# Choosing the order of 30 experts on the chip: a routed feed-forward layer whose weights are loaded from addresses in registers

## The chip, the core and the metric

The kernel runs on one core of one Trainium2 chip. The metric is the device time of one execution in microseconds (us). The core has a matrix engine (PE, with its weight loads shown apart as PEld), three other compute engines (DVE, ACT, POOL), an engine that issues transfers (SP), and 16 DMA engines that carry what SP, ACT and POOL issue. Operands lie in on-chip memory; the experts' weights lie in HBM and are read once.

## The reference

One decoder layer on 512 rows of width 1024. A mixing sublayer (pooling, RWKV-7, mLSTM, an output projection) makes `h`; it isn't touched here. Then comes a routed feed-forward sublayer with 32 experts, of which each row uses four:

```python
logits = xt @ router_w + router_b
top_val, top_idx = lax.top_k(logits, 4)
gate = jax.nn.softmax(top_val, axis=-1)
# for each expert e, over the rows that chose it:
gu = xb @ w_gu[e] + b_gu[e]                      # 1024 x 2048 weights
glu, lin = jnp.minimum(gu[:, :1024], 7.0), jnp.clip(gu[:, 1024:], -7.0, 7.0)
y_e = (glu * jax.nn.sigmoid(1.702 * glu) * (lin + 1.0)) @ w_dn[e] + b_dn[e]   # 1024 x 1024 weights
# y = sum over the four experts of gate * y_e
h = layer_norm(DEEPNORM_ALPHA * h + y, ln2_g, ln2_b)
```

With the inputs used here the experts have these numbers of rows, from expert 0 to expert 31: 69, 59, 80, 37, 61, 63, 63, 79, 48, 57, 64, 74, 77, 68, 68, 59, 75, 67, 61, 69, 39, 62, 77, 46, 60, 46, 71, 54, 74, 88, 51, 82. Fifteen of them have more than 64 rows; they are called heavy below, the other 17 light.

## The kernel before

The mixing sublayer fills the first 380 us or so. After it the program holds 32 expert steps, written out one behind the other in the order 0 to 31 (`experts`).

**Weights.** Each expert's weights are 12 chunks of 1 MiB: eight of `w_gate_up` (`load_gu`) and four of `w_down` (`load_dn`). SP issues them (L1193) into a ring of 18 buffers, in the order: gate_up of 0, gate_up of 1, down of 0, gate_up of 2, down of 1, and so on; down of 30 and down of 31 come last. An issue waits for the matmuls that read its buffer before, and, since there are eight completion lanes for SP's transfers, for the landing of the transfer eight places ahead of it. So the time of an issue that waits for a DMA is the time at which the chunk eight places ahead has landed. The addresses are constants of the program.

**Matmuls.** An expert's gathered rows (`expert_gather`, POOL, L1217) are transposed on PE; rows 0 to 63 are multiplied in `gu_low` (L1285) and in the first part of `dn` (L1331), whatever the number of rows. Rows 64 to 95 are done in `gu_high` (L1290) and `high` (L1326) only if the expert has more than 64 rows: a branch on a count, which PE, ACT and POOL each load into a register (`fill`). Experts 0 and 31 have no branch and always do both parts. `dn` of expert e runs behind the gate_up product of expert e + 1.

**Outputs.** `out` scales a result on ACT (L1335) and POOL adds it to the rows of `yd` in HBM by an indirect transfer (L1336): one for rows 0 to 63, one more for rows 64 to 95 of a heavy expert. Expert 31 is an exception: its result stays on chip (`slast`), split in a high and a low part.

**Tail.** When the additions of expert 30 have landed, POOL issues four transfers `res<-yd` (L1529, `tail_rows`), one for each block i of 128 rows, which add `yd` onto the residual `res[i]`. `tail` then does for each block: one-hot matmuls that put `slast` at its rows (L1545, L1548); for blocks 2 and 3 also a product of `res[i]` with the identity (L1543), so that PE does the addition; blocks 0 and 1 are added on DVE (L1560). Then the layer norm on ACT and DVE (L1558 to L1577) and the stores (L1578). The program text goes through the blocks from 0 to 3; the scheduler that builds the program sets the order on each engine.

**Expert 0.** While its gate_up product runs, PE also does the routing: `route_counts` (L1094, the counts of all experts by products with ones), `route_table` (L1128, the rows of each expert, by 16 products with one-hot matrices `S`), `tables` (L1174), and `out_init` for four blocks (L1140 a transpose, L1147 the down biases). `S` lies in a buffer of the ring, and the transposes and biases free others, so SP's first loads behind gate_up of expert 1 wait for these matmuls.

Of the kernel before, what the change touches and what calls it, by code (L numbers as in the profile page):

```python
# [40 lines left out]
OB = 104  # L41
PADROWS = 128

CONST_W = {}


def _consts():
    P = np.arange(128)
    cols = {}
    cols["ident"] = np.eye(128)  # L50
    strict = (P[:, None] < P[None, :]).astype(np.float64)
    incl = (P[:, None] <= P[None, :]).astype(np.float64)
# [24 lines left out]
    cols["par"] = (P[:, None] // 64 == np.arange(2)[None]).astype(np.float64)  # L77
    cols["quad"] = (P[:, None] // 32 == np.arange(4)[None]).astype(np.float64)
    cols["bd2"] = (P[:, None] // 64 == np.arange(2)[None]).astype(np.float64)
    at, parts = {}, []  # L80
    n = 0
    for k, a in cols.items():
        at[k] = (n, a.shape[1])
        n += a.shape[1]
        parts.append(a)
    return np.concatenate(parts, 1).astype(np.float32), at
# [40 lines left out]
class Trunk:  # L127
# [4 lines left out]
    def setup(self):  # L132
        nc, tc, a = self.nc, self.tc, self.a
        self.cp = cp = self.ctx.enter_context(tc.tile_pool(name="const", bufs=1))
        self.dp = self.ctx.enter_context(tc.tile_pool(name="dram", bufs=1, space=DRAM))
        self.ident = cp.tile([128, 128], F32, name="ident")
        nc.gpsimd.dma_start(self.ident, a["consts"][:, 0:128])
        self.C = cp.tile([128, CONSTS.shape[1] - 128], F32, name="cst")
        self.c = {k: self.C[:, o - 128:o - 128 + n] for k, (o, n) in CAT.items() if k != "ident"}
        e = cp.tile([128, 2], F32, name="eps")  # L140
        self.eps = {v: e[:, q:q + 1] for q, v in enumerate((1e-5, 64e-5))}
        for v, col in self.eps.items():
            nc.vector.memset(col, v)
        self.wd = self.dp.tile([6, T], F32, name="wd")
        self.tab = self.dp.tile([NE * 512, 2], F32, name="tab")
        self.hd = self.dp.tile([T + PADROWS, D], F32, name="hd")
        self.yd, self.yo = (self.dp.tile([T + PADROWS, D], F32, name=n) for n in ("yd", "yo"))

    def params(self):
        nc, a, cp = self.nc, self.a, self.sp  # L150
        self.pc = cp.tile([128, NPR], F32, name="pcol")
        nc.gpsimd.dma_start(self.pc, a["pcol"])
        nc.sync.dma_start(self.C, a["consts"][:, 128:])
# [785 lines left out]
        self.nc.scalar.dma_start(self.hd[i * 128:i * 128 + 128], r)  # L939

    def norm_params(self):
        nc, sp = self.nc, self.sp
        z = sp.tile([128, 2, 2, 128], F32, name="mkv", tag="mkv", bufs=2).rearrange("p a b c -> p (a b c)")
        self.lg = z[:, 0:128].rearrange("p (i e) -> p i e", i=NT)
        self.mk = z[:, 128:256].rearrange("p (i e) -> p i e", i=NT)
        self.v8 = z[:, 256:288].rearrange("p (i e) -> p i e", i=NT)
        self.i8 = sp.tile([128, NT, 8], U32, name="i8")
        s = self.slot("t", "ln1")
        self.lng, self.lnb = s[:, 0:1024], s[:, 1024:2048]
        for t, n in ((self.lng, "ln1_g"), (self.lnb, "ln1_b")):  # L950
            src = self.a[n]
            d = nc.scalar.dma_start(t, bass.AP(tensor=src.tensor, offset=src.offset, ap=[[0, 128], [1, D]]))
            self.after(d, self.ml_ins)
        s = self.slot("z", "slots")
# [133 lines left out]
        nc.vector.tensor_copy(self.pbs[:, i], pb)  # L1088

    def route_counts(self):  # L1090
        nc, cp = self.nc, self.cp
# [4 lines left out]
        nc.vector.tensor_copy(self.cnti, p[:, :NE])  # L1096
        self.mxi = cp.tile([128, 1], I32, name="mxi")
        mx = cp.tile([128, 1], F32, name="mx")
        nc.vector.reduce_max(mx, p[:, :NE], axis=AX.X)
        nc.vector.tensor_copy(self.mxi, mx)  # L1100


    def route_slots(self):
        nc, c = self.nc, self.c
        z = self.slot("z", "S")
# [17 lines left out]
    def route_table(self):  # L1123
        nc = self.nc
        V = self.V.rearrange("p i k e -> p (i k) e")
        p = self.tbank()
        for k in range(16):
            nc.tensor.matmul(p[0:CAP, 0:64], self.S[:, k], V[:, k], start=(k == 0), stop=(k == 15))  # L1128
        nc.vector.tensor_scalar(self.tt[:, 0:32], p[0:CAP, 0:32], self.c["pad"][0:CAP], None, OP.add)
        nc.vector.tensor_copy(self.tt[:, 32:64], p[0:CAP, 32:64])  # L1130

# [60 lines left out]
    def load(self, dst, src, gate):  # L1192
        i = self.nc.sync.dma_start(dst, src)  # L1193
        if gate is not None:
            self.after(i, gate)

    def load_gu(self, e):
        out = []
        for k in range(NK):
            w, gate = self.chunk()  # L1200
            self.load(w, self.a["w_gate_up"][e, k * 128:(k + 1) * 128], gate)
            out.append(w)
        return out

    def load_dn(self, e):
        out = []
        for k in range(0, NK, 2):
            w, gate = self.chunk()
            self.load(w.rearrange("p (k c) -> p k c", k=2), self.a["w_down"][e, k * 128:(k + 2) * 128].rearrange("(p k) c -> p k c", k=2), gate)
            out += [w[:, 0:1024], w[:, 1024:2048]]  # L1210
        return out

# [20 lines left out]

    def expert_sel(self, e):
        sel = self.mw.tile([128, 2, 128], F32R, name="sel") if e else self.cp.tile([128, 2, 128], F32R, name="sel0")
        self.nc.vector.tensor_scalar(sel[:, 0], self.c["bsel0"], 2.0 * e, None, OP.is_equal)
        self.nc.vector.tensor_scalar(sel[:, 1], self.c["bsel2"], 4.0 * e, None, OP.is_equal)  # L1237
        return sel


# [24 lines left out]


    def fill(self, e):
        if e in (0, NE - 1):
            return None
        return self.nc.values_load(self.cnti[0:1, e:e + 1], engines=[mybir.EngineType.PE, mybir.EngineType.Activation, mybir.EngineType.Pool], min_val=0, max_val=T,  # L1270
                                   skip_runtime_bounds_check_because="a count of rows, which only decides a branch")


# [90 lines left out]

    def experts(self):
        self.xg = [self.mw.tile([128, D], F32, name=f"xg{q}") for q in range(2)]
        xs, xT = {}, {0: self.first_xT()}
# [323 lines left out]
```

## Time and profile before

| | us |
|---|---|
| three timed runs | 1468.14, 1470.26, 1470.38 |
| median | 1470.26 |
| profiled execution, own time | 1465.28 |
| its span in the trace | 1463.5 |
| mean granted clock of TensorE in it | 0.976 of full |

The span is what the engines' records cover; the profiled execution's own time is 1.8 us more. All rows below come from that execution, and count from the start of its span.

### The profile page before, as it was taken

How to read it: one execution, taken by the hardware profiler on the slowest of the kernel's cores; microseconds unless marked ns; L12 is line 12 of the kernel's file. 1: busy time of each engine (PE TensorE's matmuls, PEld its weight loads, DVE VectorE, ACT ScalarE, POOL GpSimd, SP SyncE). 2: the span in 40 equal slices, each digit the busy share in tenths (PEclk: the TensorE clock that was granted, in tenths of full speed). 3: DMA queues.
4: the chain of work that ended last, by engine and by line, in shares of the span. 5: the costliest groups of instructions: out<-in, count | busy, mean ns of one | idle time of the engine just before them, and what ended most of it. 6: DMA issues, size and time to landing. Idle time of an engine off the chain costs nothing. (4 is left out here: it accounts for less than half of the span.)

```text
span 1463.5 us, 19946 instructions
## 1 busy us (share of the span) xinstructions
PE 1334.6 (91%) x7860; PEld 623.9 (43%) x7861; DVE 448.4 (31%) x1070; ACT 289.5 (20%) x617; POOL 206.8 (14%) x190
## 2 busy tenths in 40 slices
PE   7899978998999999987899999999879878899995
PEld 5677878876533333322233333333323222333323
DVE  5767687788521112111111121111111111211114
ACT  4444342453011111110001111111100100111103
POOL 1211236241001100110001111011100100010100
PEclk9999996899999999999999999999999999999998
DMA  7222233346899999999999999999999999999974
GB/s 253 73 58 72 52 79 99 132 141 269 297 364 375 396 385 403 396 390 395 403 403 397 396 398 399 406 394 394 391 389 402 394 404 395 400 395 415 408 297 118
DMA packets 95232, 461.88 MB, mean 316 GB/s; under 512 B 18084, under 2 KB 26692, under 8 KB 45962
## 3 DMA queue, kind: packets, MB, share of 16 engines
q1 hardware_dynamic: 79962, 435.61, 75.9%
q0 software_dynamic: 10592, 20.49, 6.5%
q10 hardware_dynamic: 4560, 4.15, 0.9%
q8 instruction: 82, 1.34, 0.4%
q14 instruction: 36, 0.29, 0.1%
HBM read 445.97 MB, written 18.10 MB: 317 GB/s over the span
## 5 line engine op out<-in xcount | busy, mean ns | idle before, releaser
L1285 PE MATMUL gu<-wc,xT 128*64 128x512 f32 x2048 | 486.5, 603 | 65.1 <-DMA wc<-w_gate_up 62.2
L1285 PEld LDWEIGHTS gu<-wc,xT 128*64 128x64 f32 x2048 | 143.1, 137 | 388.5 <-issue 243.1
L1298 DVE TENSOR_SCALAR glu<-gu 128x256 f32<-128x256 f32 (+1 forms) x64 | 35.6, 556 | 829.1 <-PE gu L1290 376.6
L1331 PE MATMUL dn<-wc,aT 128*64 128x512 f32 x1024 | 247.5, 603 | 4.2 <-PEq L1278 2.4
L1299 ACT ACTIVATE glu<-glu 128x256 f32<-128x256 f32 (+1 forms) x64 | 33.5, 524 | 543.1 <-DVE glu L1298 543.1
L1217 POOL DMA_INDIRECT xg<-hd,gidx x31 | 30.9, 998 | 670.8 <-PE tr L1230 660.8
L1331 PEld LDWEIGHTS dn<-wc,aT 128*64 128x64 f32 x1024 | 65.1, 136 | 118.9 <-issue 102.3
L1290 PE MATMUL gu<-wc,xT 128*32 128x512 f32 x960 | 111.5, 596 | 0.0
L1336 POOL DMA_INDIRECT yd<-eo,sidx x45 | 70.1, 1557 | 275.2 <-ACT eo L1335 275.2
L222 PE MATMUL pi<-xhi,whi 128*128 128x512 f32 x152 | 65.0, 428 | 15.9 <-ACT whi L172 8.9
L1231 ACT ACTIVATE xT<-tr 128x384 f32<-128x384 f32 x62 | 29.8, 490 | 181.1 <-PE tr L1230 181.1
L223 PE MATMUL pi<-xlo,whi 128*128 128x512 f32 x152 | 63.7, 419 | 0.5 <-DVE xlo L173 0.5
L224 PE MATMUL pi<-xhi,wlo 128*128 128x512 f32 x152 | 62.8, 413 | 0.0
L1290 PEld LDWEIGHTS gu<-wc,xT 128*32 128x32 f32 x960 | 27.0, 109 | 80.1 <-issue 79.8
L1335 ACT ACTIVATE eo<-dn,gate 128x512 f32<-128x512 f32 (+1 forms) x45 | 27.9, 621 | 163.0 <-PE dn L1331 88.9
L1326 PE MATMUL dn<-wc,aT 128*32 128x256 f32 x960 | 56.1, 381 | 1.0 <-ACT aT L1313 1.0
L173 POOL TENSOR_TENSOR wlo<-wraw,whi 128x512 fp32r<-128x512 f32 (+1 forms) x28 | 39.0, 1397 | 124.3 <-ACT whi L172 120.3
L1326 PEld LDWEIGHTS dn<-wc,aT 128*32 128x32 f32 x960 | 29.5, 110 | 34.0 <-issue 14.6
L172 ACT ACTIVATE whi<-wraw 128x512 fp32r<-128x512 f32 (+1 forms) x54 | 33.8, 634 | 47.8 <-DMA wraw<-w_in 21.9
L222 PEld LDWEIGHTS pi<-xhi,whi 128*128 128x128 f32 x152 | 30.0, 197 | 26.2 <-ACT whi L172 8.5
L1301 DVE SCALAR_TENSOR_TENSOR glu<-glu 128x256 f32<-128x256 f32 (+1 forms) x64 | 35.4, 555 | 7.2 <-ACT glu L1299 6.2
L1312 PEld LDWEIGHTS tr<-ident,glu 128*128 128x128 f32 x192 | 25.5, 208 | 26.4 <-DVE sel L1237 19.5
(489 smaller groups left out, 1501.1 us busy)
## 6 DMA issues: line engine op xcount, KB each, us to landing
wc<-w_gate_up SPq DMA_DIRECT2D x256, 1024.0 KB
wc<-w_down SPq DMA_DIRECT2D x128, 1024.0 KB
wraw<-w_in SPq DMA_DIRECT2D x46, 256.0 KB
wraw<-w_out SPq DMA_DIRECT2D x16, 256.0 KB
xraw<-xT SPq DMA_DIRECT2D x4, 512.0 KB
res<-x SPq DMA_DIRECT2D x4, 512.0 KB
hd<-res ACTq DMA_DIRECT2D x4, 512.0 KB
res<-yd POOLq DMA_DIRECT2D x4, 512.0 KB
```

Source lines behind the costliest of these rows:

```text
L172: self.hi_ins = nc.scalar.activation(hi, src, AF.Copy)
L173: return (eng or nc.vector).tensor_tensor(lo, src, hi, OP.subtract)
L222: nc.tensor.matmul(p, hi, xh, start=(k == 0), stop=False)
L223: nc.tensor.matmul(p, hi, xl, start=False, stop=False)
L224: nc.tensor.matmul(p, lo, xh, start=False, stop=(k == NK - 1))
L1285: mm(p[q][64 * h:64 * h + 64], xT[:, k, 0:64], w[:, 1024 * q + 512 * h:1024 * q + 512 * h + 512], start=False, stop=(k == NK - 1))
L1290: self.nc.tensor.matmul(p[2][32 * c:32 * c + 32], xT[:, k, 64:96], w4[:, c], start=False, stop=(k == NK - 1), skip_group_check=True)
L1298: nc.vector.tensor_scalar(out[:, c], g, 7.0, None, OP.min)
L1301: nc.vector.scalar_tensor_tensor(out[:, c], ln[:, c], 1.0, out[:, c], OP.add, OP.mult)
L1326: mm(p2[32 * c:32 * c + 32], aT[:, 4 + k % 2, 32 * (k // 2):32 * (k // 2) + 32], wd[k][:, 256 * c:256 * c + 256], start=(k == 0), stop=(k ...
L1331: mm(p0[64 * h:64 * h + 64], aT[:, k % 4, 64 * (k // 4):64 * (k // 4) + 64], wd[k][:, 512 * h:512 * h + 512], start=(k == 0), stop=(k == N ...
L1336: return nc.gpsimd.indirect_dma_start(out=self.yd.rearrange("t (c f) -> (t c) f", f=w), out_offset=bass.IndirectOffsetOnAxis(ap=self.sidx[ ...
```

## The change

The experts are put in an order by their number of rows, found on the chip. `route_counts` gets, besides the counts along a row, the counts down a column (eight small products), compares all pairs, and sums to a rank; experts 0 and 1 are kept at ranks 0 and 1. The constant `TURN` says which rank stands at which place of the program: ranks 2 to 13 alternate with ranks 14 to 25 at places 4 to 27, two others stand at places 2 and 3, and the four last ranks at places 28 to 31. With the counts above, the places have, from 0 to 31: 69, 59, 48, 51, 88, 68, 82, 67, 80, 64, 79, 63, 77, 63, 77, 62, 75, 61, 74, 61, 74, 60, 71, 59, 69, 57, 68, 54, 46, 46, 39, 37 rows. So four heavy ones stand at places 4 to 7, and from there on heavy and light ones take turns; the last four places are light.

A one-hot matrix `turn` gives the expert's number and its count for each place (`permi`) and brings the table of rows and gates into the new order by one more product. SP loads an expert's number into a register for each place from 2 on (`turn_of`) and adds it to the address of each chunk. The biases' selection compares with a column of `perm` instead of a constant. The last place now has the branch too.

```diff
+TURN = [0, 1, 27, 26] + [r for n in range(12) for r in (2 + n, 14 + n)] + [28, 29, 30, 31]
...
     def route_counts(self):
...
+        for g in range(2):
+            for i in range(NT):
+                nc.tensor.matmul(p[32 * g:32 * g + 32, 64:65], self.mkb[:, i], self.onesb[:, 0:1], start=(i == 0), stop=(i == NT - 1))
+        z = self.zS
+        key, col, self.turn, self.ttT = z[:, 1536:1568], z[0:64, 1568:1572], z[0:64, 1576:1640], z[0:64, 1640:1736]
+        no = z[0:NE, 1736:1864]
+        nc.vector.tensor_scalar(no, self.onesb[0:NE], self.cno[0:NE], None, OP.mult)
+        nc.vector.tensor_tensor(key, p[:, :NE], self.ctie, OP.add)
+        nc.vector.tensor_copy(col[:, 0:1], p[0:64, 64:65])
+        nc.vector.tensor_tensor(col[:, 1:2], col[:, 0:1], self.ctiec[0:64], OP.add)
+        nc.vector.tensor_scalar(self.turn[:, 0:NE], key[0:64], col[:, 1:2], None, OP.is_gt)
+        nc.vector.reduce_sum(col[:, 2:3], self.turn[:, 0:NE], axis=AX.X)
+        nc.vector.tensor_scalar(self.turn, self.cturn[0:64], col[:, 2:3], None, OP.is_equal)
+        q = self.tbank()
+        nc.tensor.matmul(q[:, 0:NE], no, self.turn[0:NE, 0:NE], start=True, stop=True)
+        nc.tensor.matmul(q[0:1, 64:64 + NE], col[0:NE, 0:1], self.turn[0:NE, 0:NE], start=True, stop=True)
...
     def route_table(self):
...
-            nc.tensor.matmul(p[0:CAP, 0:64], self.S[:, k], V[:, k], start=(k == 0), stop=(k == 15))
+            nc.tensor.matmul(p[0:64, 64:64 + CAP], V[:, k], self.S[:, k], start=(k == 0), stop=(k == 15))
+        tt = self.ttT
+        nc.vector.tensor_copy(tt, p[0:64, 64:64 + CAP])
+        nc.tensor.matmul(p[0:CAP, 0:64], tt, self.turn, start=True, stop=True, skip_group_check=True)
...
+    def turn_of(self, e):
+        if e < 2:
+            return slice(e, e + 1)
+        if e not in self.regs:
+            self.regs[e] = self.nc.values_load(self.permi[0:1, 0, e:e + 1], engines=[mybir.EngineType.SP], min_val=0, max_val=NE - 1,
+                                               skip_runtime_bounds_check_because="one of the experts' numbers")
+        return bass.ds(self.regs[e], 1)
+
     def load_gu(self, e):
-        out = []
+        out, x = [], self.turn_of(e)
         for k in range(NK):
             w, gate = self.chunk()
-            self.load(w, self.a["w_gate_up"][e, k * 128:(k + 1) * 128], gate)
+            self.load(w, self.a["w_gate_up"][x, k * 128:(k + 1) * 128].rearrange("o p c -> (o p) c"), gate)
...
     def fill(self, e):
-        if e in (0, NE - 1):
+        if e == 0:
             return None
-        return self.nc.values_load(self.cnti[0:1, e:e + 1], engines=[mybir.EngineType.PE, mybir.EngineType.Activation, mybir.EngineType.Pool], min_val=0, max_val=T,
+        return self.nc.values_load(self.permi[0:1, 1, e:e + 1], engines=[mybir.EngineType.PE, mybir.EngineType.Activation, mybir.EngineType.Pool], min_val=0, max_val=T,
```

**PE in the tail.** Before, behind the last matmul of expert 31, PE's program reads (`gu` and `tr` are the accumulators of blocks 0 to 2, `dn` those of block 3; `wc` holds `slast` and the one-hot matrices; DMASW1 and DMASW2 are the landings of `res<-yd` of blocks 2 and 3):

```order
L1545 MATMUL gu_9917<-wc 128x512 [waits DVE_49,Activation_49]
L1545 MATMUL gu_9918<-wc 128x512 [waits DVE_49]
L1545 MATMUL gu_9931<-wc 128x512
...
L1545 MATMUL tr<-wc 128x512 x2
L1548 MATMUL tr<-wc 128x256 x4
L1543 MATMUL tr<-res_2735,ident 128x512 [waits DMASW1_49]
L1545 MATMUL tr<-wc 128x512 x2
...
L1543 MATMUL dn_9961<-res_2735,ident 128x512 [waits DMASW2_49,PE_49]
L1545 MATMUL dn_9961<-wc 128x512 x2
```

Now the same place reads (L1594, L1596 and L1599 are the former L1543, L1545 and L1548):

```order
L1594 MATMUL dn_10087<-res_2735,ident 128x512 [waits DMASW2_49,DVE_49]
L1596 MATMUL gu_10042<-wc 128x512 [waits Activation_49]
L1596 MATMUL gu_10043<-wc 128x512
L1596 MATMUL gu_10056<-wc 128x512
L1596 MATMUL tr<-wc 128x512
L1596 MATMUL gu_10042<-wc 128x512 [waits DVE_49]
...
L1594 MATMUL tr<-res_2735,ident 128x512 [waits DMASW1_49]
L1596 MATMUL tr<-wc 128x512 x2
```

The identity product of block 3, which waits for the last of the four `res<-yd`, moved from behind blocks 0, 1 and 2 to a place ahead of all of them.

**PE in expert 0.** Before, the routing table's products and the gate_up matmuls behind the first chunk stand so:

```order
L1290 MATMUL gu_3472<-wc,xT 32x512 x4
L1128 MATMUL tr<-ohv,S 96x64 [waits DVE_49,Pool_49]
L1128 MATMUL tr<-ohv,S 96x64 x15
L1285 MATMUL gu_3470<-wc,xT 64x512 [waits DMAHW3_49]
L1174 MATMUL tr<-ohv,ident 64x64 [waits DVE_49,PE_49]
```

Now, from the last of the eight small products for the column of counts on (L1130 and L1131 make `permi`, L1170 brings the table into the new order, L1336 and L1341 are the gate_up matmuls):

```order
L1118 MATMUL tr<-onesb,mkb 32x1
L1336 MATMUL gu_3471<-wc,xT 64x512
L1336 MATMUL gu_3472<-wc,xT 64x512 x2
L1341 MATMUL gu_3473<-wc,xT 32x512
L1130 MATMUL tr<-S 128x32 [waits DVE_49,PE_49]
L1131 MATMUL tr<-S 1x32
L1167 MATMUL tr<-S,ohv 64x96 [waits Activation_49,Pool_49]
L1167 MATMUL tr<-S,ohv 64x96 x15
L1341 MATMUL gu_3473<-wc,xT 32x512 x3
L1336 MATMUL gu_3471<-wc,xT 64x512 [waits DMAHW0_49]
L1170 MATMUL tr<-S 96x64 [waits DVE_49]
```

The counts and the table moved behind parts of the second chunk, with 11 matmuls more between them; the four biases and transposes of `out_init` stand behind all of it, as before.

**SP behind expert 1's gate_up.** Before, the first down chunks and gate_up of expert 2:

```order
L1193 DMA wc<-w_down 128x2048 [waits DMAHW1_49,DMAHW5_49,DVE_49,PE_49]
L1193 DMA wc<-w_down 128x2048 [waits DMAHW2_49,PE_49]
L1193 DMA wc<-w_gate_up 128x2048 [waits DMAHW3_49,PE_49]
L1193 DMA wc<-w_gate_up 128x2048 [waits DMAHW4_49,PE_49]
L1193 DMA wc<-w_down 128x2048 [waits DVE_49,DMAHW5_49,PE_49,Pool_49]
```

Now:

```order
L1235 DMA wc<-w_down 128x2048 [waits DMAHW2_49,PE_49]
L1235 DMA wc<-w_down 128x2048 [waits DMAHW6_49,DMAHW3_49,PE_49]
L1244 TENSOR_LOAD permi [waits DVE_49]
L1235 ISA
L1235 DMA wc<-w_gate_up 128x2048 [waits DMAHW4_49,PE_49]
L1235 ISA
L1235 DMA wc<-w_gate_up 128x2048 [waits DMAHW5_49,PE_49]
```

A load of a register (one per expert) and an address computation (`ISA`, one per chunk) stand ahead of the chunks' waits on SP.

## Rows read from the trace of the kernel before

**Rows 1.** Windows of 50 us: busy time of each engine, PEclk, DMA share, GB/s

```profile
500.00:550.00 50.00, 48.44 (x222) 17.96 (x218) 6.46 (x16) 6.74 (x14) 6.66 (x5) 1.00 1.02 391
...
1350.00:1400.00 50.00, 49.12 (x334) 17.06 (x333) 4.19 (x8) 5.87 (x12) 6.76 (x5) 1.00 1.02 402
```

**Rows 2.** Timeline of SP: start us, us, instruction and count

```profile
492.90 21.19 SPq L1193 DMA_DIRECT2D wc<-w_gate_up  x8
...
1364.03 19.64 SPq L1193 DMA_DIRECT2D wc<-w_gate_up  x8
...
1407.55 0.34 SPq L1521 DMA_DIRECT2D wc<-ln_g  x1
1409.99 0.33 SPq L1521 DMA_DIRECT2D wc<-ln_b  x1
```

**Rows 3.** Waits of SP, 500 to 1400 us: total us, times, longest

```profile
SPq L1193 <- DMA wc<-w_gate_up: 526.6, 210, 4.4
...
SPq L1193 <- PEq L1278: 11.9, 3, 5.8
SPq L1193 <- PE dn L1331: 7.8, 5, 3.7
```

**Rows 4.** From the page's costliest groups: busy us, mean ns of one | idle before it

```profile
L1285 PE MATMUL gu<-wc,xT 128*64 128x512 f32 x2048 | 486.5, 603 | 65.1 <-DMA wc<-w_gate_up 62.2
```

**Rows 5.** The chain that ended last, 1400 us on: start, us, what

```profile
1422.66 5.85 DMA yd<-eo,sidx
...
1430.96 9.83 DMA res<-yd
...
1440.84 1.13 PE tr L1543 x2
```

**Rows 6.** Timeline of PE behind the last gate_up

```profile
1388.25 1.89 PE L1285 MATMUL gu<-wc,xT 128*64 128x512 f32 x8
...
1410.11 1.06 PE L1290 MATMUL gu<-wc,xT 128*32 128x512 f32 x8
...
1418.90 1.94 PE L1331 MATMUL dn<-wc,aT 128*64 128x512 f32 x8 [0.16 <-PEq L1278]
```

**Rows 7.** What the transfers to `yd` took

```profile
DMA to landing us min/median/max: 5.8/9.5/11.3
```

**Rows 8.** Timeline of PE and DVE in the tail

```profile
1433.90 1.20 PE L1545 MATMUL gu<-wc 128*128 128x512 f32 x4
...
1437.28 0.63 PE L1548 MATMUL tr<-wc 128*128 128x256 f32 x4
1437.37 0.69 DVE L1560 SCALAR_TENSOR_TENSOR res<-gu,res 128x512 f32<-128x512 f32 x1 [0.22 <-DMA res<-yd]
...
1446.14 1.02 PE L1543 MATMUL dn<-res,ident 128*128 128x512 f32 x2
...
1449.24 0.64 PE L1548 MATMUL dn<-wc 128*128 128x256 f32 x4
```

**Rows 9.** Windows of 1 or 2 us in the tail, columns as in rows 1

```profile
1438.00:1440.00 2.00, 0.00 (x0) 0.00 (x0) 2.00 (x8) 1.77 (x5) 0.00 (x0) 1.00 1.05 209
...
1442.00:1443.00 1.00, 1.00 (x5) 0.87 (x4) 0.00 (x0) 0.00 (x0) 0.00 (x0) 0.52 0.06 12
```

**Rows 10.** Window of 10 us in expert 0, columns as in rows 1

```profile
400.00:410.00 10.00, 10.00 (x43) 2.65 (x43) 3.00 (x6) 0.27 (x1) 0.00 (x0) 1.00 0.74 262
```

**Rows 11.** Timelines of PE and SP in expert 0

```profile
377.57 0.25 PE L1094 MATMUL tr<-mkb,onesb 128*128 128x32 bf16 x4 [0.52 <-DVE cst L1088]
...
382.59 2.93 PE L1128 MATMUL tr<-ohv,S 128*96 128x64 f32 x32
...
403.98 0.31 PE L1140 MATMUL tr<-ident,ohv 128*96 128x128 f32 x1
404.37 1.95 SPq L1193 DMA_DIRECT2D wc<-w_down  x2
```

**Rows 12.** Window of 5 us at the end of the weights, columns as in rows 1

```profile
1415.00:1420.00 5.00, 4.84 (x24) 1.63 (x24) 1.71 (x4) 0.00 (x0) 0.00 (x0) 1.00 0.38 155
```

More of the change, by code (lines that the diff above doesn't have):

```diff
@@ L79, in _consts @@
     cols["bd2"] = (P[:, None] // 64 == np.arange(2)[None]).astype(np.float64)
+    turn = np.full((128, 64), -1.0)
+    for g in range(2):
+        turn[32 * g:32 * g + 32, 32 * g:32 * g + 32] = TURN
+    late = np.zeros((128, 98))
+    tie = (31 - np.arange(32)) / 32.0 + 1024.0 * np.maximum(2 - np.arange(32), 0)
+    late[:, 0:64] = turn
+    late[:, 64:96] = tie[None]
+    late[:, 96] = tie[P % 32]
+    late[:, 97] = P % 32
+    cols["late"] = late
     at, parts = {}, []
@@ L137, in setup @@
         nc.gpsimd.dma_start(self.ident, a["consts"][:, 0:128])
-        self.C = cp.tile([128, CONSTS.shape[1] - 128], F32, name="cst")
-        self.c = {k: self.C[:, o - 128:o - 128 + n] for k, (o, n) in CAT.items() if k != "ident"}
+        self.C = cp.tile([128, CAT["late"][0] - 128], F32, name="cst")
+        self.c = {k: self.C[:, o - 128:o - 128 + n] for k, (o, n) in CAT.items() if k not in ("ident", "late")}
         e = cp.tile([128, 2], F32, name="eps")
@@ L152, in params @@
         nc.gpsimd.dma_start(self.pc, a["pcol"])
-        nc.sync.dma_start(self.C, a["consts"][:, 128:])
+        nc.sync.dma_start(self.C, a["consts"][:, 128:CAT["late"][0]])
         self.omm = cp.tile([128, 11], F32, name="omm")
@@ L941, in norm_params @@
     def norm_params(self):
-        nc, sp = self.nc, self.sp
+        nc, sp, c = self.nc, self.sp, self.c
         z = sp.tile([128, 2, 2, 128], F32, name="mkv", tag="mkv", bufs=2).rearrange("p a b c -> p (a b c)")
@@ L953, in norm_params @@
             self.after(d, self.ml_ins)
+        o = CAT["late"][0]
+        s = c["sel"][:, 0:98]
+        nc.sync.dma_start(s, self.a["consts"][:, o:o + 98])
+        self.cturn, self.ctie, self.ctiec, self.cno = s[:, 0:64], s[:, 64:96], s[:, 96:97], s[:, 97:98]
         s = self.slot("z", "slots")
@@ L1090, in route_counts @@
     def route_counts(self):
-        nc, cp = self.nc, self.cp
+        nc, cp, c = self.nc, self.cp, self.c
         p = self.tbank()
@@ L1098, in route_counts @@
         mx = cp.tile([128, 1], F32, name="mx")
+        for g in range(2):
+            for i in range(NT):
[13 more added lines that the diff above has]
+        nc.tensor.matmul(q[0:1, 64:64 + NE], col[0:NE, 0:1], self.turn[0:NE, 0:NE], start=True, stop=True)
+        self.perm = cp.tile([128, 2, NE], F32, name="perm")
+        self.permi = cp.tile([1, 2, NE], I32, name="permi")
+        nc.vector.tensor_copy(self.permi[:, 0], q[0:1, 0:NE])
+        nc.vector.tensor_copy(self.permi[:, 1], q[0:1, 64:64 + NE])
+        nc.vector.tensor_scalar(self.perm[:, 0], q[:, 0:NE], 2.0, None, OP.mult)
+        nc.vector.tensor_scalar(self.perm[:, 1], q[:, 0:NE], 4.0, None, OP.mult)
         nc.vector.reduce_max(mx, p[:, :NE], axis=AX.X)
@@ L1104, in route_slots @@
         nc, c = self.nc, self.c
-        z = self.slot("z", "S")
+        z = self.zS = self.slot("z", "S")
         self.S = z[:, 0:1536].rearrange("p (k s) -> p k s", k=16)
@@ L1205, in load_dn @@
     def load_dn(self, e):
-        out = []
+        out, x = [], self.turn_of(e)
         for k in range(0, NK, 2):
             w, gate = self.chunk()
-            self.load(w.rearrange("p (k c) -> p k c", k=2), self.a["w_down"][e, k * 128:(k + 2) * 128].rearrange("(p k) c -> p k c", k=2), gate)
+            self.load(w.rearrange("p (k c) -> p k c", k=2), self.a["w_down"][x, k * 128:(k + 2) * 128].rearrange("o (p k) c -> (o p) k c", k=2), gate)
             out += [w[:, 0:1024], w[:, 1024:2048]]
@@ L1235, in expert_sel @@
         sel = self.mw.tile([128, 2, 128], F32R, name="sel") if e else self.cp.tile([128, 2, 128], F32R, name="sel0")
-        self.nc.vector.tensor_scalar(sel[:, 0], self.c["bsel0"], 2.0 * e, None, OP.is_equal)
-        self.nc.vector.tensor_scalar(sel[:, 1], self.c["bsel2"], 4.0 * e, None, OP.is_equal)
+        for q, n in enumerate(("bsel0", "bsel2")):
+            self.nc.vector.tensor_scalar(sel[:, q], self.c[n], self.perm[:, q, e:e + 1] if e else 0.0, None, OP.is_equal)
         return sel
@@ L1366, in experts @@
         self.xg = [self.mw.tile([128, D], F32, name=f"xg{q}") for q in range(2)]
[L1367 removed]
+        xs, xT, self.regs = {}, {0: self.first_xT()}, {}
         wg, pend, self.added = self.load_gu(0), None, None
```

## The prediction

> **What bounds the kernel now.** I first read the windows of the expert stage. From 500 to 1400 us PE is busy almost throughout, and so are the DMA engines: their mean share is 1.02 in the first window and in the last [rows 1]. Which of the two sets the pace is told by the waits. SP issues the next gate_up chunk because an earlier one has landed: 526.6 us of waits in 210 issues, against 19.7 us in eight issues that waited for PE to free a buffer [rows 3]. PE in its turn stood 62.2 us before gate_up matmuls whose chunk had not landed [rows 4]. So the weights' transfer is the bound. Its period is read from SP's timeline: the gate_up issues that begin at 492.90 and at 1364.03 lie 26 experts apart, 33.5 us each [rows 2]. A heavy gate_up product on PE takes 22.9 us (1388.25 to 1411.17), a light one 8 x 1.94 = 15.5 us [rows 6]; no order of experts in the middle changes the number of bytes, so I expect no gain there.
>
> Then I read the end. Behind expert 31's gate_up, SP's next two issues waited only for their lanes; they show that the first two chunks of down 30 landed at 1407.55 and 1409.99, 2.44 us apart [rows 2]. By that pace the last chunk of down 30 lands at about 1414.9 and the last of down 31 at about 1424.7 (estimates). PE ends down 30 at 1418.90 + 1.94 = 1420.84 [rows 6], 4.0 us later than a PE that only follows the landings (1414.9 + 1.94 = 1416.8). The chain then runs through POOL's addition to `yd`, 5.85 us, the `res<-yd` transfers, 9.83 us from issue to the third landing, and PE's identity product of block 2 at 1440.84 [rows 5], to the end at 1463.5.
>
> **The change, part by part.**
>
> *Expert 0.* Eight products for the column of counts: four of the old kind take 0.25 us, so 0.5; two for `permi` and one that turns the table, with its copy, about 0.6 at that size. The table's 32 records take 2.93 us with 64 columns moved [rows 11]; 96 columns are worth between nothing and half as much, 1.5. Of the two ends I take 1.0, as PE's long matmuls have 603 ns for 512 columns [rows 4] and these 92 ns for 64, nearly in proportion. DVE's ranking (some ten small operations) lies beside three quarters of the second chunk; nothing to 1 us of it may stick out, 0.3 taken. What the counts cost ahead of the first chunk goes: 0.25 and 0.52 of idle [rows 11]. Sum 0.5 + 0.6 + 1.0 + 0.3 - 0.8 = +1.6, bounds +0.3 to +2.8. It moves the fourth transpose of `out_init` at 403.98, and SP's down issue at 404.37 right behind it [rows 11]. Up to then the queue has gaps (share 0.74 in 400 to 410 [rows 10]), afterwards none to hide in, so this shift stays to the last weight.
>
> *Registers.* SP's loads and address operations stand ahead of a lane's wait. SP issues in 0.34 us and a chunk lands every 2.44 [rows 2], with seven more in flight: some 2 us per chunk hide them. Nothing; beyond 2 us per chunk each further half would cost 360 x 0.5 = 180 us.
>
> *One more addition.* Expert 31's rows 64 to 81 never went to `yd`; the last place is now light, and all 15 heavy experts send a second piece of 128 KB. Four pieces of 512 KB take 9.83 us for three of them to land [rows 5], so this is worth 0.7 to 0.8. The weights' end moves by 1.6 + 0.7 = **+2.3** in all (1.0 to 3.6).
>
> *A light end.* Expert 31's gate_up no longer has the high part (22.9 to 15.5 us), so down 30 follows the landings: **-4.0** on the chain. But POOL's addition then starts while the down weights of the last place are still moving, some 6 us of them. The shortest addition took 5.8 us, the chain's own 5.85; the median of 45, nearly all beside weights, 9.5 [rows 5, 7]. Bounds 0 to +3.7, **+2.5** taken, since most of its flight lies beside weights. [...]
>
> *The tail's order on PE.* This is the largest term. Before, the one-hot matmuls of blocks 0 and 1 ran from 1433.90 to 1437.91, 4.0 us, and DVE's additions and centring beside and behind them, all while `res<-yd` was still landing; PE then stood until block 2 arrived [rows 8, 5]. Now block 3's identity product comes first, so PE stands until the fourth `res<-yd`. Blocks 1 and 2 landed by 1437.37 and 1440.84 [rows 8, 5]. The third of a 9.83 us flight is 3.3, and the DMA engines at share 1.05 carry one in some 2.6 [rows 9]; the fourth landing, call it T, is about 1443.4 (to 1444.2). Before, 20.1 us lay behind T. Now PE has behind it 4.0 for blocks 0 and 1, and 1446.14 to 1449.88 = 3.74 twice for blocks 2 and 3 [rows 8]: 11.5. [...] PE will idle over 10 us now, so I add 1.6: PE ends at T + 13.1. From PE's end to the span's end it was 13.6 (1449.88 to 1463.5) [rows 8], so T + 26.7, 6.6 more than before. ACT's squares and DVE's centring of blocks 0 and 1, which lay in the shadow of `res<-yd`, now stand in the same queues ahead of blocks 2 and 3; 0.4 for that, **+7.0**. Bounds: +5.0 if the clock holds, +9.0 if the squares (four of some 0.7 on ACT) stand wholly on the path.
>
> *Sum.* 2.3 - 4.0 + 2.5 + 7.0 = **+7.8**; bounds 1.0 - 4.0 + 0 + 5.0 = +2.0 and 3.6 - 4.0 + 3.7 + 9.0 = +12.3. The profiled execution would go from 1465.28 to 1473.1. It lies 5.0 below the median of the timed runs, so I add the difference to the median: 1470.26 + 7.8 = 1478.1, **1478**.
>
> **The rivals.**
>
> *A. No change that can be measured (0.2%, 2.9 us, either way).* The tail's new order costs little, because ACT and DVE, which own the last 13.6 us, catch up: +2 instead of 7, and the addition to `yd` isn't slowed. 2.3 - 4.0 + 0 + 2 = +0.3, 1470.6. For it: PE waits are often absorbed elsewhere. Against: blocks 2 and 3 are added by PE and ACT alone and can't start before T.
>
> *A2.* The landings don't bound the end. The mean DMA share is 0.38 in 1415 to 1420 [rows 12], as if most weights were there by 1416. Then down 30 ends 22.9 - 15.5 = 7.4 us earlier instead of 4.0, and the addition meets no weights: 2.3 - 7.4 + 0 + 7 = +1.9, 1472.2. Against: SP's issues pace the landings at 2.44 us up to 1409.99 [rows 2], with six chunks to come. [...]
>
> *B. Faster.* The order itself pays in the middle: SP waited 19.7 us for PE's buffers [rows 3]. With light experts at places 1 to 3, PE would have caught up and these waits go. If all were lost transfer time, 7.8 - 19.7 = -11.9, 1458.4; it decides from 10.7 us (7.8 + 2.9) on. Against: in 500 to 550, where SP waited so, the share is 1.02 [rows 1]; the queue was never empty.
>
> [...]
>
> **How the numbers follow.** The forecast gets 0.61, C 0.06, registers 0.02: slower 0.69. A and A2 together 0.17, the same within 0.2%. B 0.14, faster. The range leaves out B and most of C, under 0.2, and reaches down over A: 1469 to 1484; the forecast's own is 1472 to 1483.
>
> **What the trace after would show.** If right: SP's period in the middle again 33.5 us; the issues of the last layer norm's loads 1 to 4 us later; down of place 30 ended by PE 0 to 3 us before 1420.84; its addition to `yd` over 6 us; PE idle over 10 us before the product of block 3, whose wait is `res<-yd`; the one-hot matmuls of blocks 0 and 1 behind it, and some 27 us from there to the end. Wrong: a shorter period in the middle (B), PE ending down 30 at 1414 (A2), or 20 to 23 us from that landing to the end (A).

## The result and the profile after

| | before | changed |
|---|---|---|
| median of five runs, us | 1468.49 | 1476.36 |
| lowest to highest | 1461.02 to 1470.38 | 1473.45 to 1479.33 |
| profiled execution, span | 1463.5 | 1471.7 |

The changed kernel is slower: the ratio of its time to that of the kernel before is 1.0071, with a 95% interval from 1.0048 to 1.0095. A second measurement beside later experiments gave 1.0069 (1.0042 to 1.0095). The medians differ by 7.9 us, the spans by 8.2; the forecast was +7.8. The profiled execution is the fastest of the changed kernel's five.

SP's timeline of the changed kernel, from the first down chunks on, answers to [rows 2] and to the last row of [rows 11]:

```profile
408.59 0.81 SPq L1235 DMA_DIRECT2D wc<-w_down  x2
409.61 15.45 SPq L1235 DMA_DIRECT2D wc<-w_gate_up  x6
...
495.09 18.79 SPq L1235 DMA_DIRECT2D wc<-w_gate_up  x8
...
1369.48 17.72 SPq L1235 DMA_DIRECT2D wc<-w_gate_up  x8
...
1410.35 0.34 SPq L1572 DMA_DIRECT2D wc<-ln_g  x1
1412.79 0.34 SPq L1572 DMA_DIRECT2D wc<-ln_b  x1
```

Between 495.09 and 1369.48 lie 26 places of the program, as in [rows 2]: 33.6 us each, where it was 33.5. Alternating heavy and light experts gained nothing in the middle, although SP waited less for PE's buffers there. Its waits in 500 to 1400 us (total us, times, longest):

```profile
SPq L1235 <- DMA wc<-w_gate_up: 480.3, 212, 4.2
...
SPq L1235 <- PE gu L1314: 3.6, 11, 0.4
SPq L1235 <- PE dn L1377: 3.6, 6, 2.0
...
SPq L1235 <- PE dn L1382: 0.9, 3, 0.4
```

Of the two large waits of [rows 3] for PE, 19.7 us together, 0.9 us is left, with 3.6 us for another line of `dn` (L1377). All of SP's waits for PE in this stretch went from 26.1 to 11.0 us. The waits for landings became shorter too, and the first chunk of the last eight still lands 2.8 us later than before (1410.35 against 1407.55, the issues of `ln_g`): SP's waits were no loss of the transfer.

The end is read from the chain of the changed kernel, which answers to [rows 5]:

```profile
1417.82 1.95 PE dn L1382 x8
...
1420.72 0.59 ACT eo L1386
...
1421.58 8.10 DMA yd<-eo,sidx
...
1429.74 1.38 issue
1431.12 1.25 POOL res L1580 x2
...
1432.84 11.42 DMA res<-yd
...
1444.39 2.05 PE dn L1594 x2
```

PE ends down 30 at 1419.77 (1417.82 + 1.95) instead of 1420.84. The addition to `yd` takes 8.10 us instead of 5.85. The wait behind it is now for the fourth `res<-yd` (11.42 us) and not for the third. Then PE's timeline, with the rows that answer to [rows 8]:

```profile
1444.39 2.05 PE L1594 MATMUL dn<-res,ident 128*128 128x512 f32 x2 [14.38 <-DMA res<-yd]
1445.45 2.27 PE L1596 MATMUL gu<-wc 128*128 128x512 f32 x3
...
1450.65 1.02 PE L1594 MATMUL tr<-res,ident 128*128 128x512 f32 x2
...
1456.46 0.64 PE L1599 MATMUL dn<-wc 128*128 128x256 f32 x4
```

PE stood 14.38 us ahead of block 3's product (the product of one of its two halves; the other half still stands behind block 2), and only then began blocks 0 and 1, which before were done while it waited. From the landing at 1444.3 to the end of the span are 27.4 us; before, by the estimate of the prediction, 20.1. The experiment with the new tail order on the kernel before shows below that this estimate was too low: 21.6. The windows of 1 us show the clock behind that wait (PEclk is the third number from the right):

```profile
1444.00:1445.00 1.00, 0.61 (x1) 0.50 (x2) 0.00 (x0) 0.00 (x0) 0.00 (x0) 0.50 0.00 0
...
1447.00:1448.00 1.00, 1.00 (x4) 0.77 (x3) 0.00 (x0) 0.00 (x0) 0.00 (x0) 0.67 0.00 0
1448.00:1449.00 1.00, 1.00 (x9) 0.92 (x9) 0.27 (x1) 0.00 (x0) 0.00 (x0) 1.00 0.00 0
```

It is at 0.50 as PE resumes (called the lower clock below), 0.67 in the mean of the fourth window, and 1.00 from 1448 on.

### The profile page after: what moved, and what is told of

Same layout as the page of the kernel before. It is cut to its first block, busy times and chain, and to the rows that moved or that the text cites. A ratio compares the mean times of both kernels' runs of the same rounds, so it can differ in the third digit from the quotient of the medians.

```text
span 1471.7 us, 20755 instructions
## 1 busy us (share of the span) xinstructions
PE 1332.7 (91%) x7874; PEld 625.1 (42%) x7875; DVE 452.3 (31%) x1082; ACT 289.3 (20%) x618; POOL 210.4 (14%) x191
## 5 line engine op out<-in xcount | busy, mean ns | idle before, releaser
L1336 PE MATMUL gu<-wc,xT 128*64 128x512 f32 x2048 | 482.7, 599 | 63.2 <-DMA wc<-w_gate_up 60.9
L1336 PEld LDWEIGHTS gu<-wc,xT 128*64 128x64 f32 x2048 | 141.5, 136 | 384.4 <-issue 225.2
L1350 ACT ACTIVATE glu<-glu 128x256 f32<-128x256 f32 (+1 forms) x64 | 33.5, 524 | 534.9 <-DVE glu L1349 534.8
L1341 PE MATMUL gu<-wc,xT 128*32 128x512 f32 x960 | 112.5, 596 | 0.0
L1341 PEld LDWEIGHTS gu<-wc,xT 128*32 128x32 f32 x960 | 27.8, 109 | 79.3 <-issue 78.1
L1377 PE MATMUL dn<-wc,aT 128*32 128x256 f32 x960 | 54.9, 381 | 0.0
L1377 PEld LDWEIGHTS dn<-wc,aT 128*32 128x32 f32 x960 | 29.7, 110 | 30.2 <-issue 12.2
L235 PEld LDWEIGHTS pi<-xhi,whi 128*128 128x128 f32 x152 | 29.6, 195 | 26.1 <-ACT whi L185 8.5
```

The costliest lines, as they stand in the source:

```text
L235: nc.tensor.matmul(p, hi, xh, start=(k == 0), stop=False)
L1336: mm(p[q][64 * h:64 * h + 64], xT[:, k, 0:64], w[:, 1024 * q + 512 * h:1024 * q + 512 * h + 512], start=False, stop=(k == NK - 1))
L1341: self.nc.tensor.matmul(p[2][32 * c:32 * c + 32], xT[:, k, 64:96], w4[:, c], start=False, stop=(k == NK - 1), skip_group_check=True)
L1377: mm(p2[32 * c:32 * c + 32], aT[:, 4 + k % 2, 32 * (k // 2):32 * (k // 2) + 32], wd[k][:, 256 * c:256 * c + 256], start=(k == 0), stop=(k ...
```

## The experiments

The theory: the time is lost in the tail, by PE's order there (7 us), and a little in expert 0 (2 to 3 us); the light end gains 4 us on PE and loses most of it to a longer addition; the middle is bound by the transfer and indifferent to the order. Rivals: ACT and DVE own the tail whatever PE does; registers on SP cost time in the middle; the alternating order gains there.

Each ratio is against runs of the kernel before on the same chip. All ratios in the table were measured with 12 runs of the kernel, but for the changed one (5 and 6). A useful yardstick in each trace is the stretch from the issue of `ln_g` (the landing of the first chunk of down 30) to the end of the span, since it leaves out all differences that arise ahead of the end. It is one execution each, so ratios and traces need not agree to a microsecond.

| kernel | `ln_g` | span | from there to the end | ratio to before, interval |
|---|---|---|---|---|
| before | 1407.55 | 1463.5 | 55.95 | |
| changed | 1410.35 | 1471.7 | 61.35 | 1.0071 (1.0048 to 1.0095) |
| changed, once more | 1412.63 | 1475.4 | 62.77 | 1.0069 (1.0042 to 1.0095) |
| old tail order on the change | 1405.47 | 1460.9 | 55.43 | 1.0008 (0.9992 to 1.0025) |
| new tail order on before | 1407.52 | 1470.5 | 62.98 | 1.0038 (1.0018 to 1.0058) |
| machinery, own order | 1412.66 | 1466.2 | 53.54 | 1.0019 (1.0003 to 1.0035) |
| order, no machinery | 1410.29 | 1466.0 | 55.71 | 0.9989 (0.9975 to 1.0002) |
| plain loads, before | 1407.63 | 1463.4 | 55.77 | 0.9999 (0.9983 to 1.0016) |
| plain loads, changed | 1414.76 | 1468.4 | 53.64 | 1.0006 (0.9988 to 1.0024) |
| plain loads and POOL, before | 1408.81 | 1462.5 | 53.69 | 0.9982 (0.9967 to 0.9997) |
| plain loads and POOL, changed | 1412.09 | 1461.4 | 49.31 | 0.9984 (0.9966 to 1.0001) |

### The old tail order on the changed kernel

```diff
                 if i > 1:
-                    mm(p, self.ident, self.res[i][:, hs[q]], start=True, stop=False)
+                    x = mm(p, self.ident, self.res[i][:, hs[q]], start=True, stop=False)
+                    if i == 3:
+                        self.after(x, last)
...
+            if i == 2:
+                last = y
```

Here `y` is the latest matmul of the block, so `last` is the last one of block 2, and both halves of block 3's product are put behind it.

> The changed kernel, with block 3's identity product put back behind blocks 0, 1 and 2 on PE; nothing else. If PE's order in the tail costs the 7 us that the prediction gave it (7.2 by the two traces: 27.4 us from the fourth res<-yd to the end instead of 20.2), then the landing stays at about 1444, PE runs the one-hot matmuls of blocks 0 and 1 right behind the last place's down product (about 1431 to 1435), the rest takes 20 to 21 us, and the time is 1469 to 1470, the same as before the change within 0.2%. If ACT and DVE own the end anyway, the gain is under 3 us (above 1473).

Median 1466.73 beside 1466.68 of before, as expected for PE's order as the cost. The stretch at the end is 55.43 us, 5.9 to 7.3 less than in the two traces of the changed kernel, and PE waits for block 2 again:

```profile
1437.07 2.07 PE L1594 MATMUL tr<-res,ident 128*128 128x512 f32 x2 [7.11 <-DMA res<-yd]
```

So nearly the whole loss of the change is where one product stands on PE. The rival that ACT and DVE own the tail falls.

### The new tail order on the kernel before

```diff
+        early = self.mps.tile([128, 512], F32, name="dn2")
+        lead = mm(early, self.ident, self.res[3][:, hs[1]], start=True, stop=False)
         for i in range(NT):
...
                 for z in range(2):
-                    mm(p, self.P[q][:, t], self.slast[z], start=i < 2 and z == 0, stop=False)
+                    x = mm(p, self.P[q][:, t], self.slast[z], start=i < 2 and z == 0, stop=False)
+                    if i < 2:
+                        self.after(x, lead)
```

> The kernel before, with one identity product of block 3 put ahead of blocks 0, 1 and 2 on PE, as the change does; no order of experts, no registers. If PE's order is the cost by itself: 6 to 8 us slower than before, PE idle for some 9 us ahead of that product, 26 to 28 us from it to the end. If the 7 us in the changed kernel came from something else near the end (a late addition to yd, the light last place): within 2 us of before.

1.0038: 5.6 us slower by the ratio (2.6 to 8.5), a little under the 6 to 8 expected; by the traces the end grows from 55.95 to 62.98, 7.0 us. PE's first row there:

```profile
1442.02 2.04 PE L1538 MATMUL dn<-res,ident 128*128 128x512 f32 x2 [8.11 <-DMA res<-yd]
```

A cost of the same size, without registers or a new order of experts. From this product to the end of the span are 28.5 us. As the product waits for the fourth `res<-yd`, its start also dates that landing on the kernel before: 1441.9, where the prediction estimated 1443.4. Then 21.6 us lay behind the landing before (1463.5 - 1441.9), and 27.4 behind it in the first trace of the change, 5.8 more.

### The machinery alone, and the order alone

Own order, with the machinery:

```diff
-TURN = [0, 1, 27, 26] + [r for n in range(12) for r in (2 + n, 14 + n)] + [28, 29, 30, 31]
+TURN = list(range(32))
...
-        nc.vector.tensor_scalar(self.turn, self.cturn[0:64], col[:, 2:3], None, OP.is_equal)
+        nc.vector.tensor_scalar(self.turn, self.cturn[0:64], self.cno[0:64], None, OP.is_equal)
```

> The changed kernel with all its machinery (column of counts, permi, registers on SP, the branch in the last place), but the place of each expert is its own number, so the order is that of before, and PE's tail is in the old order. The comparison's result replaces the rank; the ranking is still computed. If the machinery costs only the delay of expert 0: weights end 1.5 to 2.8 us later than before, the middle as before, 2 to 3 us slower in all (1470.5 to 1471.5 where before has 1468.5). If address registers or the loads on SP cost in the middle: over 5 us, with a longer period per expert.

The new order as constants in the kernel before (both with the old tail order):

```diff
+ORD = [0, 1, 8, 30, 29, 14, 31, 17, 2, 10, 7, 5, 12, 6, 22, 21, 16, 4, 11, 18, 28, 24, 26, 15, 19, 9, 13, 27, 23, 25, 20, 3]
...
-            self.load(w, self.a["w_gate_up"][e, k * 128:(k + 1) * 128], gate)
+            self.load(w, self.a["w_gate_up"][ORD[e], k * 128:(k + 1) * 128], gate)
```

> The kernel before, with the experts in the order that the change finds, but written into the program as constants for these inputs: no ranking, no registers, the old PE order in the tail; the last place has the branch. If the order is worth only what the prediction said: the down product of place 30 ends 3 to 4 us earlier, its addition to yd takes 2 to 3.7 us longer, one more addition costs 0.7, so -1 us, between -2.5 and +1.5. If alternating heavy and light experts pays in the middle (the rival with 19.7 us of waits): 5 us faster or more, with the landings of the last weights that much earlier.

The machinery costs 0.19%, 2.8 us; the order gains 0.11%, 1.6 us, not clear of zero. Neither the registers nor the alternation shows in the middle: the period over 26 places is 33.5 us with the machinery and 33.6 with the order. In the order alone the chain has what was foreseen for the light end:

```profile
1420.67 0.59 ACT eo L1337
...
1421.52 8.06 DMA yd<-eo,sidx
...
1432.21 10.05 DMA res<-yd
```

The kernel before has, in the same chain and for the two halves of block 2 on PE:

```profile
1421.80 0.59 ACT eo L1335
```

```profile
1440.84 1.13 PE L1543 MATMUL tr<-res,ident 128*128 128x512 f32 x2 [2.92 <-DMA res<-yd]
...
1443.30 1.91 PE L1543 MATMUL tr<-res,ident 128*128 128x512 f32 x2
```

In the order alone these halves are:

```profile
1442.31 2.08 PE L1545 MATMUL tr<-res,ident 128*128 128x512 f32 x2 [7.51 <-DMA res<-yd]
...
1445.89 1.91 PE L1545 MATMUL tr<-res,ident 128*128 128x512 f32 x2
```

Counted from `ln_g` (1410.29), ACT's scaling starts after 10.4 us; before after 14.25 (1421.80 from 1407.55). PE's lag of 3.9 us is gone, but the addition takes 2.2 us more, and PE, waiting longer for block 2, works on it at the lower clock (0.50 from 1442 to 1448; two products take 2.08 us at 1442.31, 1.02 at 1448.75): its second half begins 3.6 us behind the first, 2.46 before. This trace is of the slowest of the twelve runs, so its end, 55.71, shows less of the gain than the ratio does.

### The changed kernel once more

> The changed kernel as it is, once more, beside the next ones on one chip. The parts measured apart sum to +0.38% (the tail's order) + 0.19% (the machinery) - 0.11% (the order of experts) = +0.46%, 6.8 us. If the parts are all there is: ratio 1.003 to 1.006. If they act on each other (a light last place leaves PE idle longer ahead of the late product): 1.006 or more.

1.0069. The parts above sum to 0.46%, so this is above the sum. The excess lies with the late product: the change with the old tail order (1.0008) is what machinery and order give together (0.19% - 0.11%), while the late product adds 0.38% to the kernel before and undoing it takes 0.61 to 0.63%, some 9 us, off the change. The intervals of the four measurements together are wide enough to hold the difference, and by the traces the tail alone cost 5.9 to 7.3 us on the change and 7.0 on before. Whether the parts act on each other stays open.

The two traces of the changed kernel differ at the end by 1.4 us (61.35 and 62.77), and also in the time at the lower clock. In the first, PE worked 3.2 us at 0.50 behind its wait; in the second it was 5.8 us, as PE's first row and the windows show:

```profile
1446.94 2.05 PE L1594 MATMUL dn<-res,ident 128*128 128x512 f32 x2 [14.65 <-DMA res<-yd]
```

```profile
1451.00:1452.00 1.00, 1.00 (x6) 1.00 (x5) 0.00 (x0) 0.00 (x0) 0.00 (x0) 0.50 0.00 0
...
1453.00:1454.00 1.00, 1.00 (x8) 0.92 (x8) 0.84 (x3) 0.00 (x0) 0.00 (x0) 1.00 0.00 0
```

With the new tail order on the kernel before it was 5.5 us (1442.0 to 1447.5), and from the late product to the end 28.5 us, as here.

### The addition to `yd` without weights beside it

```diff
-                    wd = self.load_dn(e)
+                    wd = self.load_dn(e) if e < NE - 1 else None
...
             if e == NE - 1:
+                wd = self.load_dn(e, self.added)
                 self.tail_rows()
```

With it each of these issues waits for the landing of place 30's addition.

> The changed kernel with the old PE order in the tail; the last place's four down chunks are issued only when place 30's addition to yd has landed, so nothing else is in the queues while it runs. If the weights beside it lengthened the addition (5.85 before, 8.1 in the changed kernel): 5.2 to 6.2 us from issue to landing. If it is something of the new order (the table's rows, POOL): 8 us again. The weights then end some 10 us later and the whole is 5 to 15 us longer; that isn't the question.

The timeline of POOL and SP there:

```profile
1420.29 1.55 POOL L1389 DMA_INDIRECT yd<-eo,sidx  x1 [29.80 <-ACT eo L1388]
1425.41 2.10 SPq L1235 DMA_DIRECT2D wc<-w_down  x4
```

SP's down chunks, which wait for the landing, are issued 5.1 us behind the addition. Beside the last chunks it took 8.05 to 8.11 us in the changed kernel, in the one with the old tail order, in the order alone and with the plain loads. So the weights cost it 3.0 us. The kernel as a whole took 1476.34 us in the one run that was made, as the weights came late.

### Two versions that take the additions off POOL's queue

First, SP loads blocks 2 and 3 of `yd` plainly, and PE adds them:

```diff
         for i in range(NT):
-            self.nc.gpsimd.dma_start(self.res[i], self.yd[i * 128:i * 128 + 128], accum_op=OP.add)
+            if i < 2:
+                self.nc.gpsimd.dma_start(self.res[i], self.yd[i * 128:i * 128 + 128], accum_op=OP.add)
+            else:
+                self.nc.sync.dma_start(self.yt[i], self.yd[i * 128:i * 128 + 128])
...
+                if i > 1:
+                    mm(p, self.ident, self.yt[i][:, hs[q]], start=False, stop=True)
```

> The kernel before, but blocks 2 and 3 of yd are not added onto the residual by POOL's transfers: SP loads them as they are into a free buffer, and PE adds them by one more identity product each half. If the wait for res<-yd is what holds the tail: blocks 2 and 3 are there 2 to 4 us earlier, PE doesn't idle long enough for its clock to sink, 3 to 5 us faster than before (0.2 to 0.35%). If PE (four products of 0.5 us more) or DVE and ACT bound the tail: within 2 us of before.

> The same edit on the changed kernel. Block 3's first product is still first in PE's order, but it now multiplies the residual, which waits for no transfer of the tail; the landed blocks of yd come last in their blocks. If the loss of the change was that wait: 8 to 12 us faster than the changed kernel, and 2 to 5 us faster than before. If the order ahead of blocks 0 and 1 costs for another reason: no better than the changed kernel by more than 4 us.

On the kernel before: no gain (0.9999), and the expectation was wrong. DVE's third addition, block 1, shows why:

```profile
1437.69 0.69 DVE L1567 SCALAR_TENSOR_TENSOR res<-gu,res 128x512 f32<-128x512 f32 x1 [2.57 <-DMA res<-yd]
...
1440.64 0.69 DVE L1567 SCALAR_TENSOR_TENSOR res<-gu,res 128x512 f32<-128x512 f32 x1 [1.64 <-DMA res<-yd]
```

Block 1 came at 1440.6, where it was there by 1437.37 [rows 8]: beside SP's two loads, issued 0.4 us ahead of POOL's first addition, POOL's second transfer landed 3 us later. On the changed kernel the same edit takes 9 us off (1.0069 to 1.0006), as its late product now waits for no transfer. It doesn't get below before, where 2 to 5 us faster was expected.

Second, SP loads all four blocks plainly, and POOL adds blocks 0 and 1 on the chip:

```diff
...
+            self.nc.sync.dma_start(self.yt[i], self.yd[i * 128:i * 128 + 128])
+        for i in range(2):
+            for f in (slice(0, 512), slice(512, 1024)):
+                self.nc.gpsimd.tensor_tensor(self.res[i][:, f], self.res[i][:, f], self.yt[i][:, f], OP.add)
...
```

> The kernel before; SP loads all four blocks of yd as they are, POOL adds blocks 0 and 1 onto the residual on the chip (four operations of some 1.4 us), PE blocks 2 and 3 by one more identity product each half. Where the first of these versions lost was block 1's transfer with addition, landing 3 us later behind SP's two loads; that is gone here. PE, which starts the one-hot matmuls behind a heavy last expert, is the next limit: it ends 1 to 2 us earlier than before, so 1 to 3 us faster than before, hardly to be told from no change.

> The same on the changed kernel, with its order of experts and all its machinery. The last place is light, so PE starts the one-hot matmuls some 3 us earlier, and nothing in the tail waits for a transfer with addition: 10 to 15 us faster than the changed kernel, 3 to 6 us faster than before (0.2 to 0.4%). If the light end is worth nothing: the same as the version on the kernel before plus the 2.8 us of the machinery.

0.9982 on the kernel before and 0.9984 on the changed one: 2.6 and 2.4 us below before. The first one's interval ends below 1, the second one's just above it. On the kernel before, this is within the expected 1 to 3 us; on the changed one 3 to 6 us were expected, so that one fell short. The end is 2.3 us shorter than before in the one, and 6.6 us shorter in the other (49.31 against 55.95): with nothing in the tail waiting for an addition by transfer, the light end is worth 4.4 us in the traces. But `ln_g` comes 3.3 us later in the second (1412.09 against 1408.81), and by the ratios nothing of the 4.4 us is left.

## Why the prediction was right, point by point

The total is nearer than its terms: +2.8 at `ln_g`, where +2.3 was forecast, and +5.4 from there to the end in the first trace, where -4.0 + 2.5 + 7.0 = +5.5 was. The mechanisms hold. That the sum came out within half a microsecond is in part luck, as errors offset each other in expert 0, at the light end and in the tail.

**Bound and middle: right.** The period stayed, and the rival B, that the order pays there, is refuted by the order alone (-1.6 us, not clear of zero, where B asked for up to -19.7) and by SP's lost waits that moved no landing forward.

**Expert 0: mis-sized.** The term was +1.6 us, bounds +0.3 to +2.8. SP's six gate_up chunks of expert 2 start at 409.61 instead of 406.37: +3.2, outside the bounds. (Expert 0 doesn't start at the same time in every trace: its first gate_up product is at 379.73 before, at 378.42 and 380.83 in the two traces of the changed kernel. Counted from there it is 31.2 us in both of these against 26.6 before, +4.6; of this 0.8 is the earlier start that the term allowed for, so the term itself is worth 3.8.) PE's rows show what the sum left out, first now, then before:

```profile
378.42 1.94 PE L1336 MATMUL gu<-wc,xT 128*64 128x512 f32 x8
380.29 1.07 PE L1341 MATMUL gu<-wc,xT 128*32 128x512 f32 x8
...
382.49 0.27 PE L1118 MATMUL tr<-onesb,mkb 128*32 128x1 bf16 x8
...
384.54 1.04 PE L1341 MATMUL gu<-wc,xT 128*32 128x512 f32 x2
385.52 0.40 PE L1130 MATMUL tr<-S 32*128 32x32 f32 x2
385.85 0.22 PE L1131 MATMUL tr<-S 32*1 32x32 f32 x2
386.00 2.85 PE L1167 MATMUL tr<-S,ohv 128*64 128x96 f32 x32
388.78 1.06 PE L1341 MATMUL gu<-wc,xT 128*32 128x512 f32 x6
...
405.72 0.32 PE L1182 MATMUL tr<-ident,ohv 128*96 128x128 f32 x1
405.96 1.93 PE L1336 MATMUL gu<-wc,xT 128*64 128x512 f32 x6
407.82 0.74 PE L1189 MATMUL tr<-bdn,GT 96*128 96x512 f32 x2
```

```profile
379.73 1.94 PE L1285 MATMUL gu<-wc,xT 128*64 128x512 f32 x8
...
405.22 0.74 PE L1147 MATMUL tr<-bdn,GT 96*128 96x512 f32 x2
```

```profile
406.37 17.04 SPq L1193 DMA_DIRECT2D wc<-w_gate_up  x6
```

The prices of the new products were right or too high: 0.27 for the eight, 0.62 for `permi`, and 96 columns cost nothing (2.85 against 2.93 us). The fourth transpose is 1.74 us later (405.72 against 403.98), near the forecast, but in part because expert 0 started 1.3 us earlier in this trace; counted from its first product it is 3.05 later. The new products are about 1 us of that. The other 2.0 come from a split: a group of eight records of L1341 takes 1.07 us, and where the new order on PE puts other products into its midst, the first two take 1.04 and the last six 1.06. This happens twice (again from 398.33 on), and not before the change. The fourth pair of biases, at 407.82, moreover stands behind six gate_up records, 1.9 us, where there were two, 1.0 us (405.22 before), which makes it 2.6 us later. Before, SP issued one down chunk behind the transpose and only the second one (405.99) behind the biases; now it issues both behind the biases, from 408.59 on, which adds the other 0.6. The prediction priced the new products and followed one instruction; it left out what the new order does to the products around them and the queue behind.

**"This shift stays to the last weight": not quite.** +3.2 and the one more addition arrive as +2.8 at `ln_g`; from the issue at 406.37 or 409.61 to `ln_g` are 1001.2 us before and 1000.7 after. The 0.7 us of the addition doesn't show: this stretch varies by more from trace to trace, from 1000.1 to 1002.0 us in kernels with the code of before up to there. The forecast of that end, +2.3, was near because two errors offset each other.

**The light end: its two terms right, the whole not.** -4.0 forecast; counted from `ln_g`, PE ends down 30 at 13.3 us before and 9.4 now, -3.9. The addition: +2.5 forecast, +2.25 measured, within its bounds of 0 to 3.7. That weights beside it lengthen it was the forecast's reading of the spread in [rows 7]; the addition alone (5.1 us against 8.1) bears it out, and block 1's transfer, 3 us later beside SP's loads, agrees. But in the order alone, which has the light end without the late product, the end is only 0.2 us shorter than before (55.71 against 55.95), not the 1.5 of these two terms. The sum had no term for 0.9 us more on POOL (below, under what was left out), nor for the 1.1 us that block 2 lost at the lower clock.

**The tail's order: right in mechanism, near in size.** +7.0 forecast; by the traces 5.9 to 7.3 by undoing it and 7.0 by doing it alone, by the ratios some 9 and 5.6. The wait and the order behind the landing came as written; from the landing to the end 27.4 us, forecast 26.7 and 0.4 for ACT's and DVE's queues. The 1.6 us added in it for PE's long idle is shown by no run behind such an idle: on the kernel before block 2 took 5.3 us (1440.84 to 1446.14, clock 0.50 to 0.52 from 1442 to 1445) behind 2.92 us of idle, against 3.74 for block 3 [rows 5, 8]. In the trace after, PE worked 3.2 us at 0.50 and ended 12.7 us behind the start of its first product (1444.39 to 1457.10), where the sum had 13.1. Two errors lie in the size. The fourth landing of before was put at 1443.4, 1.5 us too late; the forecast's own [rows 9] speak against it, as the DMA share is 0.06 from 1442 to 1443. And what lies behind the landing was put at 27.1, where the three traces have 27.4, 28.5 and 28.5, the last two with 5.5 to 5.8 us at the lower clock. They offset each other.

**Left out.** POOL takes 1.4 us from the addition's landing to its next issue where the last place is light (the `issue` piece in the chain above), and 0.5 where it isn't. The cause wasn't tried.

**Which rival came nearest.** A asked for a tail where ACT and DVE absorb the wait; undoing the order shows that they don't. A2 put the end of down 30 on PE at 1414, as if the weights were there early. It came at 1419.77, and the last chunk of the last place landed just before 1428.08, when PE began on it, though the mean DMA share was down to 0.18 in 1427 to 1428:

```profile
1428.08 1.94 PE L1382 MATMUL dn<-wc,aT 128*64 128x512 f32 x8 [0.91 <-DMA wc<-w_down]
```

The lower clock didn't last through the tail either: PE worked at 0.50 for 3.2 to 5.8 us of the 27.4 to 28.5 behind the landing.

## What to carry to other kernels

A change of data order can move an instruction that nobody touched: read what the scheduler made of the tail on each engine, and look for a wait that now stands ahead of work which used to hide it. Where a transfer bounds the middle, as here, look for what an order of the work can pay at the end, where the transfer runs out. And when a step gets later, follow what stands behind it in its engine's queue, not only the step.

## What the runs showed of the hardware that was not expected

- The clock at a short idle: before, PE idled 2.92 us ahead of block 2, and the granted clock was 0.50 to 0.52 from 1442 to 1445. With the machinery and the old order of experts PE idled 2.61 us at the same place (one trace each), and all windows from 1444 to 1450 show 1.00; block 2 took 3.7 us there (1444.97 to 1448.66) instead of 5.3, which is most of why its end is 2.4 us shorter:

```profile
1444.97 1.13 PE L1594 MATMUL tr<-res,ident 128*128 128x512 f32 x2 [2.61 <-DMA res<-yd]
```

```profile
1445.00:1446.00 1.00, 1.00 (x3) 0.52 (x4) 1.00 (x2) 1.00 (x3) 0.00 (x0) 1.00 1.07 213
```

- Behind a long idle the lower clock (0.50) lasted differently long: 3.2 us of work behind 14.38 us of idle, 5.8 behind 14.65 in a second trace of the same kernel, 5.5 behind 8.11.
- An addition by transfer of 64 rows took 5.1 us alone, 8.1 beside the last weights; over the stage, pieces of 64 and of 32 rows together, it was 9.5 in the median [rows 7].
- Beside two plain loads of 512 KB, issued by SP just ahead of POOL's adding transfers, the second of these landed 3 us later.
- Eight gate_up records with 32 stationary columns took 1.07 us in a row; split by other products into two and six, they took 1.04 and 1.06.
- PE's 32 records with 96 columns and 64 stationary ones took 2.85 us, those with 64 columns and 96 stationary ones 2.93.
